# Two heads' 64-column matmuls on the two column halves of the array, and a different order of the down products between two token halves

## The chip, the cores and the metric

The kernel runs on one core of one Trainium2 chip. The metric is the device time of one execution in microseconds (us); lower is better. PE is TensorE (PEld its weight loads), DVE is VectorE, ACT is ScalarE, POOL is GpSimd, SP is SyncE.

## The reference, cut to what matters

One layer of a hybrid decoder for 1024 prompt tokens and 8 decode tokens. After an input projection, half of the channels go through a pooling mixer, the other half through RWKV-7 time mixing, which keeps one 64x64 state S per head (8 heads):

```python
def step(S, inp):
    r_t, w_t, k_t, v_t, aa_t, bb_t = inp
    sa = jnp.einsum('bhvk,bhk->bhv', S, aa_t)
    S = S * w_t[:, :, None, :] + sa[..., None] * bb_t[:, :, None, :] + v_t[..., None] * k_t[:, :, None, :]
    return S, jnp.einsum('bhvk,bhk->bhv', S, r_t)
...
mix = jnp.concatenate([pool_out, rwkv_out], axis=-1).astype(x.dtype) @ w_out
x = x + mix.astype(x.dtype)
h2 = _rmsnorm(x, norm2_g)
x = x + (jnp.square(jax.nn.relu(h2 @ w_up)) @ w_down).astype(x.dtype)
```

A final RMSNorm follows. The widths are 1024 (model) and 4096 (MLP).

## The kernel before

Activations lie transposed, channels on partitions, tokens along the free dimension. There are two stages that matter here.

**The mixer stage** (to about 530 us). The time mixing is done in chunks of 64 tokens. A `Unit` is a pair of heads (`hp`, 0 to 3) and a half of the prompt (512 tokens, 8 chunks), so there are 8 units and 64 chunks. `rkv` and `stage1` prepare a unit, `inverse` inverts its chunks' triangular matrices into `TT`, and `chain` (L578 to L624) walks through its chunks in order, because each chunk needs the state that the chunk before it left in `SV`. In a chunk the two heads of the pair stand in the two halves of the partitions (`R[0]`, `R[1]`). One f32 matmul handles both heads at once: 128 weight columns, 128 moving columns, of which only the two diagonal 64x64 blocks of the result are read. The chain of a chunk is:

1. `pq` (L601) and the first half of `py` (L602) from the state `SV`;
2. ACT copies `pq` to `Q`;
3. `pa` (L605) multiplies `Q` by `TT`;
4. ACT copies the diagonal blocks of `pa` into `SV`, one instruction per head;
5. `pu` (L608) and the second half of `py` (L609);
6. DVE (L617) makes the next chunk's state from `pu`, one instruction per head.

The profile shows every f32 matmul as two passes (x2), each with its own weight load, and every `fp32r` matmul as one. A tuple `128*128` in its rows is the part of the array that an instruction takes (rows*columns). The scheduler mixes other units' matmuls between the chain's: projections (`pj`, fp32r, some 258 columns), `sc` (L431), transposes (`bkt`, L445). The order per engine is fixed when the program is built, and each engine works in that order.

**The MLP stage** (from about 627 us). Half 0 is the first 512 tokens, half 1 the other 520. `up_pair(p)` makes two blocks of the hidden layer with seven products `b0` to `b6` (L1014, 12 matmuls each). Its raw weights `a11`, `a21`, `a22`, `a12` have one buffer each and are loaded by SP (L985); ACT and DVE split them into two fp32r parts (`wh`, `wl`), DVE adds them (L991), adds the products up (L1029), and ACT and DVE write the results `uh`, `ul` (L1025). `down(g, m)` adds one output block of hidden group g (L1080, 12 matmuls `dn` over half 0, 24 over half 1). `downs(G, ...)` is a generator of such blocks; `up_pair` takes one of them after each of its second to fifth product. Groups 0 to 7 belong to half 0, 8 to 15 to half 1. At G == 7, `open_operands(1)` reloads the 14 operand tiles of `up_pair` (520 KB each, queue of POOL) for half 1; a tile is free once half 0's last pair (15) has used it. Group 7's down products need the results of pair 15.

Of the kernel before, what the change touches and what calls it, by code (L numbers as in the profile page):

```python
# [1 line left out]

# [1 line left out]

# [82 lines left out]
def _build(ctx, nc, tc, I, O, dbg):  # L87
# [5 lines left out]
    def act(out, in_, func=AF.Copy, bias=0.0, scale=1.0, **k):  # L93
        A.activation(out, in_, func, bias=bias, scale=scale, **k)  # L94
# [483 lines left out]
    def chain(U):  # L578
        hp = U.hp
        z1 = Zt[U.half][2]  # L580
        for i in range(2):
            nm = f"{hp}_{2 * U.half + i}"
            AR, RB, BKT, SV, TT = U.AR[i], U.RB[i], U.BKT[i], U.SV[i], U.TT
            if i == 0:
                for h in range(2):
                    if U.half == 0:
                        GP.memset(SV[R[h], 0, h, :], 0.0)
                    else:
                        act(SV[R[h], 0, h, :], Sf[hp][R[h], :])
            pyp = ps_y.tile([P, 512], F32, tag="y", name=f"py{nm}")  # L590
            py = pyp.rearrange("p (c h t) -> p c h t", h=2, t=64)
            for c in range(4):
                g = 4 * i + c
                gn = f"{U.nm}_{g}"
                sg = rcp.tile([P, 2, 64], F32, tag="sg", name=f"sg{gn}", bufs=2)
                act(sg, SV[:, c, :, :], scale=U.gam[:, g:g + 1])

                o = 256 * (hp % 2)
                pq, pa = (pcs[:, o + 128 * q:o + 128 * q + 128].rearrange("p (h t) -> p h t", t=64) for q in range(2))
                pu = pq  # L600
                PE.matmul(pq, AR[:, c, 0, :, :], SV[:, c, :, :], start=True, stop=True)  # L601
                PE.matmul(py[:, c, :, :], SV[:, c, :, :], AR[:, c, 1, :, :], start=True, stop=False)  # L602
                Q = rcp.tile([P, 2, 64], F32, tag="Q", name=f"Q{gn}", bufs=2)
                act(Q, pq)
                PE.matmul(pa, TT[:, g, :, :], Q, start=True, stop=True)  # L605
                for h in range(2):
                    act(SV[R[h], c, h, :], pa[R[h], h, :])
                PE.matmul(pu, BKT[:, c, :, :], SV[:, c, :, :], start=True, stop=True)  # L608
                PE.matmul(py[:, c, :, :], SV[:, c, :, :], RB[:, c, :, :], start=False, stop=True)  # L609
                for h in range(2):  # L610
                    if g == 7:
                        dst = Sf[hp][R[h], :]
                    elif c == 3:
                        dst = U.SV[1][R[h], 0, h, :]
                    else:
                        dst = SV[R[h], c + 1, h, :]
                    V.scalar_tensor_tensor(dst, pu[R[h], h, :], U.gam[R[h], g:g + 1], sg[R[h], h, :], ALU.mult, ALU.add)  # L617
            ys = rcp.tile([P, 256], F32, tag="ys", name=f"ys{nm}", bufs=2)
            for h in range(2):
                act(ys[R[h]].rearrange("p (c t) -> p c t", t=64), py[R[h], :, h, :])  # L620
            post(hp, nm, pyp, ys, 256, U.bv[:, 256 * i:256 * i + 256], z1[:, 256 * i:256 * i + 256], ys)
            QM.dma_start(mix_d[4 + hp][U.half][:, 256 * i:256 * i + 256], ys)
        if U.half:
            QM.dma_start(O["wkv_p"][hp], Sf[hp])  # L624
# [484 lines left out]
    for G in range(15):  # L1109
# [6 lines left out]
        if G == 7:  # L1116
            open_operands(1)
            for _ in first:
                pass
        up_pair(2 * G + 2, rest if G == 7 else first)  # L1120
        up_pair(2 * G + 3, () if G == 7 else rest)
        if G == 7:
            for c in (0, 256):
                ss = ps_m.tile([P, 512], F32, tag="m", name=f"ss30{c}")[:, :256]
                acc = tmp(f"acc30{c}", "acc")[:, :256]
# [104 lines left out]
```

## Time and profile before

| what | value |
|---|---|
| time before, median of 3 runs | 1336.7 us (1336.37 to 1336.93) |
| profiled execution, its own time | 1335.81 us |
| its span in the trace | 1334.0 us |
| PE busy | 1267.3 us, 95% |
| DVE busy | 1050.9 us, 79% |
| ACT busy | 822.5 us, 62% |
| mean granted TensorE clock | 0.991 |

A busy share is an average over stages. The matmuls are pipelined: a row's duration runs from its start to its modelled end and overlaps the next one, so the pace of PE is read from the distance between starts, not from durations.

### The profile page before, as it was taken

What the parts mean: (1) busy time and instruction counts of PE and PEld (TensorE: products, weight loads), DVE (VectorE), ACT (ScalarE), POOL (GpSimd) and SP (SyncE); (2) the same over time, 40 slices, a digit from 0 to 9 for tenths busy, and PEclk for the clock granted to TensorE, in tenths of its full rate; (3) what the DMA queues carried; (4) which work ended last, traced back from release to release, by engine and by line L of the source; (5) the groups of instructions that cost most, each with busy time, mean ns of one, the idle gap of its engine ahead of it and who ended that gap; (6) DMA issues with size and microseconds to landing.
All of it is one profiled execution on the core that took longest, in us unless ns stands there. A gap on an engine that the chain in (4) does not pass through costs nothing.

```text
span 1334.0 us, 27179 instructions
## 1 busy us (share of the span) xinstructions
PE 1267.3 (95%) x10230; PEld 1146.4 (86%) x10230; DVE 1050.9 (79%) x2331; ACT 822.5 (62%) x2015; POOL 125.4 (9%) x248
## 2 busy tenths in 40 slices
PE   5999999899999989989999999999899999999996
PEld 5987788798777867789989888998799999999996
DVE  8897687778877756589989997786698787878775
ACT  7668677776777657364757564555465645455552
POOL 4101001210011021110002320001000000000000
PEclk9999999999999989999999999999899999999999
DMA  6323123222222253442335663335634323332321
GB/s 209 102 54 83 43 50 90 95 93 53 66 56 48 63 164 135 142 149 80 119 115 150 181 167 96 113 97 186 217 99 147 103 89 105 94 106 93 104 71 64
DMA packets 119492, 143.19 MB, mean 107 GB/s; under 512 B 55769, under 2 KB 71257, under 8 KB 119353
## 3 DMA queue, kind: packets, MB, share of 16 engines
q1 hardware_dynamic: 97184, 92.22, 23.7%
q0 software_dynamic: 20320, 47.39, 11.4%
q10 hardware_dynamic: 1856, 1.85, 0.4%
q8 instruction: 80, 1.31, 0.4%
q14 instruction: 52, 0.42, 0.1%
HBM read 120.68 MB, written 20.97 MB: 106 GB/s over the span
## 4 chain that ended last, share of the span: by engine, by line
PE 68%; ACT 12%; DVE 11%; DMA 5%; issue 4%; POOL 1%; SPq 0%; DVEq 0%; ACTq 0%; POOLq 0%
PE dn L185 23%; PE b L1014 21%; PE pj L185 8%; PE mx L185 4%; ACT SV L94 2%; DMA a<-in_w_up 2%; PE pcs L608 1%; PE sc L431 1%; ACT wh L94 1%; ACT TT L94 1%; PE pcs L605 1%; DVE tm L525 1%; PE pcs L601 1%; DVE wl L167 1%; PE bkt L445 1%
## 5 line engine op out<-in xcount | busy, mean ns | idle before, releaser
L185 PE MATMUL dn<-uh,wh 128*128 128x260 f32 (+1 forms) x736 | 237.7, 324 | 6.1 <-DVE x L1080 4.3
L185 PE MATMUL dn<-ul,wh 128*128 128x260 f32 (+1 forms) x736 | 237.4, 323 | 1.2 <-DVE ul L1025 1.2
L185 PE MATMUL dn<-uh,wl 128*128 128x260 f32 (+1 forms) x736 | 237.2, 323 | 1.0 <-DVE wl L167 1.0
L94 ACT ACTIVATE wh<-a 128x512 fp32r<-128x512 f32 x192 | 120.8, 629 | 161.3 <-PE dn L185 85.0
L94 ACT ACTIVATE wh<-wr 128x512 fp32r<-128x512 f32 x230 | 142.9, 622 | 98.6 <-PE dn L185 26.0
L185 PE MATMUL pj<-xh,wh 128*128 128x258 f32 (+3 forms) x576 | 172.3, 299 | 13.7 <-ACT wh L94 13.7
L167 DVE TENSOR_TENSOR wl<-wr,wh 128x512 fp32r<-128x512 f32 x230 | 155.7, 681 | 35.4 <-ACT wh L94 27.5
L185 PE MATMUL pj<-xl,wh 128*128 128x258 f32 (+3 forms) x576 | 170.3, 296 | 0.0
L185 PE MATMUL pj<-xh,wl 128*128 128x258 f32 (+3 forms) x576 | 170.0, 295 | 0.1
L185 PEld LDWEIGHTS dn<-uh,wh 128*128 128x128 f32 x736 | 138.9, 189 | 17.3 <-ACT uh L94 3.2
L185 PEld LDWEIGHTS dn<-uh,wl 128*128 128x128 f32 x736 | 138.8, 189 | 12.3 <-DVE wl L167 1.2
L185 PEld LDWEIGHTS dn<-ul,wh 128*128 128x128 f32 x736 | 138.9, 189 | 10.8 <-DVE ul L1025 1.8
L176 DVE TENSOR_TENSOR wl<-a,wh 128x512 fp32r<-128x512 f32 x192 | 131.3, 684 | 6.2 <-ACT wh L94 3.6
L1080 DVE TENSOR_TENSOR x<-dn,x 128x260 f32<-128x260 f32 (+1 forms) x192 | 97.6, 511 | 41.5 <-PE dn L185 39.9
L185 PEld LDWEIGHTS pj<-xh,wh 128*128 128x128 f32 x576 | 109.9, 191 | 17.6 <-ACT wh L94 13.7
L185 PEld LDWEIGHTS pj<-xl,wh 128*128 128x128 f32 x576 | 110.0, 191 | 2.3 <-issue 1.9
L185 PEld LDWEIGHTS pj<-xh,wl 128*128 128x128 f32 x576 | 109.8, 191 | 1.8 <-issue 1.0
L94 ACT ACTIVATE c<-c 128x256 f32<-128x256 f32 (+1 forms) x128 | 53.1, 415 | 45.7 <-DVE c L1029 45.2
L991 DVE TENSOR_TENSOR a<-a,a 128x512 f32<-128x512 f32 x96 | 66.2, 689 | 19.0 <-DMA a<-in_w_up 17.5
L1025 DVE TENSOR_TENSOR ul<-u,uh 128x256 fp32r<-128x256 f32 (+1 forms) x128 | 53.6, 423 | 18.8 <-ACT uh L94 18.4
L185 PE MATMUL mx<-mh,wh 128*128 128x260 f32 (+1 forms) x192 | 64.9, 341 | 3.3 <-ACT mh L94 1.9
L185 PE MATMUL mx<-ml,wh 128*128 128x260 f32 (+1 forms) x192 | 63.6, 332 | 0.9 <-DVE ml L881 0.9
(421 smaller groups left out, 3388.6 us busy)
## 6 DMA issues: line engine op xcount, KB each, us to landing
a<-in_w_up SPq DMA_DIRECT2D x128, 256.0 KB, 2.6
wr<-in_w_down SPq DMA_DIRECT2D x128, 256.0 KB, 2.6
wr<-in_w_in POOLq DMA_DIRECT2D x72, 256.0 KB, 3.1
wr<-in_w_out POOLq DMA_DIRECT2D x26, 256.0 KB, 3.2
xr<-in_xT SPq DMA_DIRECT2D x16, 256.0 KB, 3.6
mr<-mix SPq DMA_DIRECT2D x8, 260.0 KB, 4.3
x<-in_xT SPq DMA_DIRECT2D x4, 520.0 KB, 5.0
blk<-AA SPq DMA_DIRECT2D x16, 128.0 KB, 2.7
```

The lines of the kernel that those rows point to most:

```text
L94: A.activation(out, in_, func, bias=bias, scale=scale, **k)
L167: V.tensor_tensor(l[:, :w], raw[:, :w], f32(h[:, :w]), op=ALU.subtract)
L176: V.tensor_tensor(l, raw, f32(h), op=ALU.subtract)
L185: PE.matmul(ps, lhs, rhs, start=i == 0, stop=i == n - 1)
L431: PE.matmul(psc[:, c, :], BK[:, c, 2 * h:2 * h + 2, :], AR[:, c, :, h, :], start=True, stop=True)
L445: PE.transpose(pt[:, c, :], BK[:, c, 2 * h:2 * h + 2, :].rearrange("p a t -> p (a t)"), ident)
L525: V.tensor_tensor(pr[:, q], l[:, q].unsqueeze(2).to_broadcast([64, m, m, m]), r[:, q].rearrange("p k j -> p j k").unsqueeze(1).to_broadcas ...
L601: PE.matmul(pq, AR[:, c, 0, :, :], SV[:, c, :, :], start=True, stop=True)
L991: V.tensor_tensor(a[out], a[x], a[y], op=op)
L1014: PE.matmul(ps, lhs[:, c], rhs, start=k == i == 0, stop=k == 3 and i == 2)
L1025: V.tensor_tensor(ul, u, f32(uh), op=ALU.subtract)
L1080: V.tensor_tensor(d, ps[:, :n], d, op=ALU.add)
```

## The change

In `chain`, the four matmuls whose result is wanted only on the diagonal are written once per head: the weights are the 64 columns of one head and the result goes to that head's half of the partitions, which is the tile position (0, 0) or (0, 64) of a 128*64 tile. `pa` stays one matmul on the full array with 64 moving columns instead of 128. `Q` and `py` become half as wide, and the output copy `ys` one instruction on 128 partitions instead of two on 64.

In the MLP loop, pair 15 takes only two of group 6's last four down products between its own; the other two follow it. At G == 7 all eight down products of the group come ahead of pair 16, and pairs 16 and 17 run without any. The final norm of half 0 moves from G == 7 to G == 9.

```diff
--- before.py
+++ after.py
@@ -1,4 +1,5 @@
 from contextlib import ExitStack
+from itertools import islice
 
 import numpy as np
 
@@ -588,7 +589,7 @@
                     else:
                         act(SV[R[h], 0, h, :], Sf[hp][R[h], :])
             pyp = ps_y.tile([P, 512], F32, tag="y", name=f"py{nm}")
-            py = pyp.rearrange("p (c h t) -> p c h t", h=2, t=64)
+            py = pyp[:, 0:256].rearrange("p (c t) -> p c t", t=64)
             for c in range(4):
                 g = 4 * i + c
                 gn = f"{U.nm}_{g}"
@@ -596,17 +597,20 @@
                 act(sg, SV[:, c, :, :], scale=U.gam[:, g:g + 1])
 
                 o = 256 * (hp % 2)
-                pq, pa = (pcs[:, o + 128 * q:o + 128 * q + 128].rearrange("p (h t) -> p h t", t=64) for q in range(2))
-                pu = pq
-                PE.matmul(pq, AR[:, c, 0, :, :], SV[:, c, :, :], start=True, stop=True)
-                PE.matmul(py[:, c, :, :], SV[:, c, :, :], AR[:, c, 1, :, :], start=True, stop=False)
-                Q = rcp.tile([P, 2, 64], F32, tag="Q", name=f"Q{gn}", bufs=2)
+                pq, pa, pu = (pcs[:, o + 64 * q:o + 64 * q + 64] for q in range(3))
+                for h in range(2):
+                    PE.matmul(pq[R[h]], AR[:, c, 0, h, :], SV[:, c, h, :], start=True, stop=True)
+                for h in range(2):
+                    PE.matmul(py[R[h], c, :], SV[:, c, h, :], AR[:, c, 1, h, :], start=True, stop=False)
+                Q = rcp.tile([P, 64], F32, tag="Q", name=f"Q{gn}", bufs=2)
                 act(Q, pq)
                 PE.matmul(pa, TT[:, g, :, :], Q, start=True, stop=True)
                 for h in range(2):
-                    act(SV[R[h], c, h, :], pa[R[h], h, :])
-                PE.matmul(pu, BKT[:, c, :, :], SV[:, c, :, :], start=True, stop=True)
-                PE.matmul(py[:, c, :, :], SV[:, c, :, :], RB[:, c, :, :], start=False, stop=True)
+                    act(SV[R[h], c, h, :], pa[R[h]])
+                for h in range(2):
+                    PE.matmul(pu[R[h]], BKT[:, c, h, :], SV[:, c, h, :], start=True, stop=True)
+                for h in range(2):
+                    PE.matmul(py[R[h], c, :], SV[:, c, h, :], RB[:, c, h, :], start=False, stop=True)
                 for h in range(2):
                     if g == 7:
                         dst = Sf[hp][R[h], :]
@@ -614,10 +618,9 @@
                         dst = U.SV[1][R[h], 0, h, :]
                     else:
                         dst = SV[R[h], c + 1, h, :]
-                    V.scalar_tensor_tensor(dst, pu[R[h], h, :], U.gam[R[h], g:g + 1], sg[R[h], h, :], ALU.mult, ALU.add)
+                    V.scalar_tensor_tensor(dst, pu[R[h]], U.gam[R[h], g:g + 1], sg[R[h], h, :], ALU.mult, ALU.add)
             ys = rcp.tile([P, 256], F32, tag="ys", name=f"ys{nm}", bufs=2)
-            for h in range(2):
-                act(ys[R[h]].rearrange("p (c t) -> p c t", t=64), py[R[h], :, h, :])
+            act(ys, pyp[:, 0:256])
             post(hp, nm, pyp, ys, 256, U.bv[:, 256 * i:256 * i + 256], z1[:, 256 * i:256 * i + 256], ys)
             QM.dma_start(mix_d[4 + hp][U.half][:, 256 * i:256 * i + 256], ys)
         if U.half:
@@ -1117,9 +1120,13 @@
             open_operands(1)
             for _ in first:
                 pass
-        up_pair(2 * G + 2, rest if G == 7 else first)
-        up_pair(2 * G + 3, () if G == 7 else rest)
-        if G == 7:
+            for _ in rest:
+                pass
+        up_pair(2 * G + 2, first)
+        up_pair(2 * G + 3, islice(rest, 2) if G == 6 else rest)
+        for _ in rest:
+            pass
+        if G == 9:
             for c in (0, 256):
                 ss = ps_m.tile([P, 512], F32, tag="m", name=f"ss30{c}")[:, :256]
                 acc = tmp(f"acc30{c}", "acc")[:, :256]
```

The built program has 9123 matmuls instead of 8867. In their order PE enters the 128*64 shape 187 times, against 4 times before (the 4 belong to the decode tokens, L705), and leaves it as often.

On PE, a chunk of heads 2 and 3 (unit 1_0, third chunk) before; `sc` is another unit's work:

```order
L431 MATMUL sc2_1_1_1745<-AR1_138,BK_145 128x128
L601 MATMUL pcs_108<-SV1_0_1223,AR2_139 128x128
L602 MATMUL py1_0_1922<-AR2_139,SV1_0_1223 128x128
L431 MATMUL sc2_1_1_1745<-AR1_138,BK_145 128x128
L605 MATMUL pcs_108<-Q1_0_2_1953,TT1_158 128x128
L431 MATMUL sc2_1_1_1745<-AR1_138,BK_145 128x128 x2
L608 MATMUL pcs_108<-SV1_0_1223,BKT1_0_1222 128x128
L609 MATMUL py1_0_1922<-RB2_143,SV1_0_1223 128x128
```

The same chunk in the changed kernel (line numbers are higher by one to three; `pj` and `bkt` are other units' work, `py` with L604 is the first and with L613 the second half of the output):

```order
L604 MATMUL py1_0_1952<-AR2_139,SV1_0_1223 64x64
L446 MATMUL bkt2_1_0_1785<-cst_86,BK_145 128x128 x2
L602 MATMUL pcs_108<-SV1_0_1223,AR2_139 64x64 x2
L604 MATMUL py1_0_1952<-AR2_139,SV1_0_1223 64x64
L186 MATMUL pj15_0_2271<-xh0_171,wl_2268 128x256
...
L446 MATMUL bkt2_1_1_1791<-cst_86,BK_145 128x128
L607 MATMUL pcs_108<-Q1_0_2_1993,TT1_158 128x64
L446 MATMUL bkt2_1_1_1791<-cst_86,BK_145 128x128 x3
L613 MATMUL py1_0_1952<-RB2_143,SV1_0_1223 64x64
L611 MATMUL pcs_108<-SV1_0_1223,BKT1_0_1222 64x64 x2
L613 MATMUL py1_0_1952<-RB2_143,SV1_0_1223 64x64
```

One head's `py` of L604 now stands apart from the group of three behind it, with transposes between, so that the chunk enters the 128*64 shape three times: at the first L604, at L602, and at L613.

On DVE, in pair 15 before (`a..._16` are raw weights of pair 16, `x10<-dn6_5` adds a down product of group 6):

```order
L176 TENSOR_TENSOR wl_11984<-a22_15_11786,wh_11983 128x512
L1080 TENSOR_TENSOR x10_6510<-dn6_5_0_11883,x10_6510 128x512
L176 TENSOR_TENSOR wl_12008<-a12_15_11788,wh_12007 128x512
L991 TENSOR_TENSOR a21_16_12144<-a21_16_12144,a22_16_12146 128x512
L1029 TENSOR_TENSOR u3_15_11914<-u2_15_11875,b3_15_11897 128x256
L167 TENSOR_TENSOR wl_12061<-wr_12058,wh_12060 128x512
L1080 TENSOR_TENSOR x10_6510<-dn6_6_0_11922,x10_6510 128x512
L167 TENSOR_TENSOR wl_12081<-wr_12078,wh_12080 128x512
L1029 TENSOR_TENSOR u4_15_11953<-u2_15_11875,b4_15_11936 128x256
```

The same place in the changed kernel:

```order
L177 TENSOR_TENSOR wl_12184<-a22_15_12026,wh_12183 128x512
L994 TENSOR_TENSOR as3_16_12494<-a11_16_12462,a21_16_12464 128x512
L1083 TENSOR_TENSOR x10_6750<-dn6_4_0_12084,x10_6750 128x512
L177 TENSOR_TENSOR wl_12208<-a12_15_12028,wh_12207 128x512
L1032 TENSOR_TENSOR u2_15_12115<-p1_15_12047,b2_15_12098 128x256
L994 TENSOR_TENSOR a21_16_12464<-a21_16_12464,a22_16_12466 128x512
L168 TENSOR_TENSOR wl_12233<-wr_12230,wh_12232 128x512
L1083 TENSOR_TENSOR x10_6750<-dn6_5_0_12123,x10_6750 128x512
L168 TENSOR_TENSOR wl_12253<-wr_12250,wh_12252 128x512
L1032 TENSOR_TENSOR u3_15_12154<-u2_15_12115,b3_15_12137 128x256
```

The addition that needs `a22_16` still stands among pair 15's additions, between `u2` and `u3`. The split of `a22_15`, whose end frees the buffer for `a22_16`, has moved ahead of `as3_16`, the addition that needs `a21_16` (before it stood behind it), and four rows lie between it and the addition of `a22_16` instead of two.

On DVE, the end of pair 15 before (`x10<-dn7_0` is the first use of group 7's first down product):

```order
L1025 TENSOR_TENSOR ul31_11781<-u10_15_12001,uh31_11780 128x256
L1029 TENSOR_TENSOR c12_15_12023<-u4_15_11953,b6_15_12006 128x256
L176 TENSOR_TENSOR wl_12171<-a12_16_12148,wh_12170 128x512
L991 TENSOR_TENSOR a12_16_12148<-a12_16_12148,a11_16_12142 128x512
L1025 TENSOR_TENSOR ul30_11779<-u01_15_12025,uh30_11778 128x256
L1080 TENSOR_TENSOR x10_6510<-dn7_0_0_12064,x10_6510 128x512
```

And in the changed kernel:

```order
L1032 TENSOR_TENSOR c12_15_12223<-u4_15_12173,b6_15_12206 128x256
L168 TENSOR_TENSOR wl_12361<-wr_12358,wh_12360 128x512
L1083 TENSOR_TENSOR x10_6750<-dn6_6_0_12236,x10_6750 128x512
L168 TENSOR_TENSOR wl_12381<-wr_12378,wh_12380 128x512
L1028 TENSOR_TENSOR ul30_12019<-u00_15_12073,uh30_12018 128x256
L1028 TENSOR_TENSOR ul30_12019<-u01_15_12225,uh30_12018 128x256
L1028 TENSOR_TENSOR ul31_12021<-u11_15_12177,uh31_12020 128x256
L1028 TENSOR_TENSOR ul31_12021<-u10_15_12201,uh31_12020 128x256
L1083 TENSOR_TENSOR x10_6750<-dn6_7_0_12256,x10_6750 128x512
L168 TENSOR_TENSOR wl_12401<-wr_12398,wh_12400 128x512
L1083 TENSOR_TENSOR x10_6750<-dn7_0_0_12304,x10_6750 128x512
```

Two down products of group 6 and the splits of further down weights now lie between the last sum `c12` of pair 15 and group 7's first down product; two additions for pair 16 no longer do.

## Rows read from the trace of the kernel before

**Rows 1.** the first line of the page: the profiled execution's span.

```profile
span 1334.0 us, 27179 instructions
```

**Rows 2.** busy time by stage; (x) counts instructions; last columns clock, DMA share, GB/s.

```profile
66.00:530.00 464.00, 436.75 (x4281) 370.00 (x4280) 350.28 (x858) 334.77 (x957) 57.17 (x116) 0.99 0.29 78
...
640.00:940.00 300.00, 298.41 (x1864) 267.09 (x1864) 247.66 (x496) 175.74 (x385) 35.25 (x67) 1.00 0.47 141
...
1030.00:1300.00 270.00, 269.99 (x2252) 269.74 (x2251) 212.15 (x428) 147.45 (x305) 0.00 (x0) 1.00 0.31 96
```

**Rows 3.** timeline of PE over one chunk: start us, duration us, instruction, xcount.

```profile
151.32 0.43 PE L601 MATMUL pcs<-SV,AR 128*128 128x128 f32 x2
...
151.81 0.39 PE L431 MATMUL sc<-AR,BK 128*128 128x128 f32 x2
152.13 0.49 PE L605 MATMUL pcs<-Q,TT 128*128 128x128 f32 x2
152.46 0.61 PE L431 MATMUL sc<-AR,BK 128*128 128x128 f32 x4
153.16 0.49 PE L608 MATMUL pcs<-SV,BKT 128*128 128x128 f32 x2
153.48 0.39 PE L609 MATMUL py<-RB,SV 128*128 128x128 f32 x2
...
153.95 0.60 PE L445 MATMUL bkt<-cst,BK 128*128 128x128 f32 x4
...
154.51 0.39 PE L601 MATMUL pcs<-SV,AR 128*128 128x128 f32 x2
```

**Rows 4.** instructions on tile pcs on ACT: duration ns min/median/max.

```profile
L94 ACT ACTIVATE SV<-pcs x128: 197/219/222, 106.7 to 519.7; 64x64 f32<-64x64 f32 x128
...
L94 ACT ACTIVATE Q<-pcs x64: 254/278/287, 68.0 to 518.4; 128x128 f32<-128x128 f32 x64
```

**Rows 5.** timeline of PE around 16 matmul passes that use 64 columns.

```profile
533.65 0.39 PE L185 MATMUL mx<-mh,wh 128*128 128x512 f32 x1
533.88 0.40 PE L185 MATMUL mx<-ml,wh 128*128 128x512 f32 x1
534.20 1.09 PE L705 MATMUL dpa<-r,dS 128*64 128x2 f32 x16
535.23 0.50 PE L185 MATMUL mx<-mh,wl 128*128 128x512 f32 x1
535.56 0.40 PE L185 MATMUL mx<-mh,wh 128*128 128x512 f32 x1
```

**Rows 6.** timeline of weight loads: those of the same 16 passes.

```profile
534.20 1.01 PEld L705 LDWEIGHTS dpa<-r,dS 128*64 128x64 f32 x16 [0.36 <-ACT dX L94]
```

**Rows 7.** timeline of weight loads: 32 passes that alternate between two 32x32 tiles.

```profile
102.00 0.58 PEld L565 LDWEIGHTS pi<-XB,AA 32*32 32x32 f32 x32 [0.86 <-DVE XB L560]
```

**Rows 8.** instructions on tile ys: the two copies of a segment's output.

```profile
L94 ACT ACTIVATE ys<-py x32: 364/379/381, 119.0 to 521.2; 64x256 f32<-64x256 f32 x32
```

**Rows 9.** timeline of PE before group 7's down products; [idle before <-releaser].

```profile
941.78 0.47 PE L185 MATMUL dn<-uh,wh 128*128 128x512 f32 x1 [0.67 <-DVE x L1080]
...
945.45 0.48 PE L185 MATMUL dn<-uh,wh 128*128 128x512 f32 x1 [2.04 <-DVE x L1080]
...
949.76 1.22 PE L185 MATMUL dn<-uh,wh 128*128 128x512 f32 x2 [1.78 <-ACT uh L94]
...
953.06 0.39 PE L185 MATMUL dn<-uh,wl 128*128 128x512 f32 x1
```

**Rows 10.** timeline of DVE ahead of that: its two longest pauses.

```profile
931.55 0.69 DVE L991 TENSOR_TENSOR as<-a,a 128x512 f32<-128x512 f32 x1 [4.57 <-issue]
...
939.41 0.69 DVE L991 TENSOR_TENSOR a<-a,a 128x512 f32<-128x512 f32 x1 [5.03 <-DMA a<-in_w_up]
```

**Rows 11.** busy time by stretch around that place.

```profile
920.00:950.00 30.00, 25.51 (x146) 21.56 (x145) 17.50 (x34) 13.68 (x29) 7.42 (x14) 0.93 1.01 336
...
960.00:990.00 30.00, 30.00 (x207) 27.89 (x206) 25.47 (x50) 19.13 (x41) 0.00 (x0) 1.00 0.27 84
```

## The prediction, on record before the changed kernel ran

> **What bounds the kernel now.** The profiled execution took 1335.8 us by its own time, 0.9 us under the median of the runs; its span is 1334.0 us [rows 1]. I read first where PE, the engine with the highest busy share, is really paced by its own work, and for that the busy time by stage [rows 2]. From 1030 to 1300 us PE is busy for all of 270 us with 2252 passes, 0.12 us each: nothing there can be gained by moving other engines' work. The same holds almost wholly from 640 to 940. In the mixer stage, 66 to 530 us, PE's row says 437 of 464 us busy, but matmul durations overlap, and this share hides lost time. So I went to the timeline of one chunk of the chain [rows 3] and counted starts. A pass of 128 f32 columns paces at (0.61 - 0.39)/2 = 0.11 us (rows with x4 and x2). The chunk lasts from one L601 to the next, 3.19 us. Against that pace PE loses 0.05 us between L601 and the `sc` passes behind L602 (0.49 for four passes), 0.10 ahead of L605 (0.32 for two), 0.11 in L605, 0.26 ahead of L608 (0.70 for four) and 0.10 in L608: 0.62 us. These are waits of the chain, for `Q`, for the copies into `SV` and for weight loads that cannot run ahead of an operand that isn't there. Over 64 chunks that is some 40 us. The third place is the gap ahead of group 7's down products [rows 9].
>
> **The change, part 1: the chain.** Four terms.
>
> *Matmul time.* Now ten passes a chunk, 10 x 0.11 = 1.10 us. After: 16 passes of 64 columns and two of `pa`, which load 128 weight columns each as before and keep 0.11. The trace has 64-column passes: 16 of them have their weight loads within 1.01 us [rows 6], so some 0.06 us each, all on the same half of the columns. If the halves run in line, a chunk has 16 x 0.06 + 0.22 = 1.18 us, 5 us more over 64 chunks. If every pass overlaps with one of the other half, 0.48 + 0.22 = 0.70, 26 us less. Tiles do overlap where they differ in rows and in columns: 32 loads of 32 columns that alternate between two such tiles take 0.58 us [rows 7], 0.018 each, where half of 0.06 would be 0.03. Halves of the columns with the same rows are not in the trace. The order rows show how much can overlap: of eight matmuls a chunk only the two of L602 stand directly side by side for both heads; one L604 stands alone, and L613, L611, L611, L613 come as head 0, 0, 1, 1, so that only their middle can overlap. That is about 0.18 us less than in line, 1.00 us, or 6 us less than now. I take this, -6, and keep -26 and +5 as ends.
>
> *Changes of shape.* PE enters the `128*64` shape 183 times more, and leaves it as often. Around the 64-column passes that exist [rows 5] the pace of the matmuls ahead is 0.23 us; the first pass starts 0.32 us behind the last of them, 0.09 late. Behind the last pass the next matmul starts some 0.08 us late (16 x 0.06 from 534.20 is 535.16, it starts at 535.23) and the one behind it after 0.33 instead of 0.23, 0.10 late. A round trip costs 0.27 us: nothing of the next shape, not even its weights, seems to start until the passes of the old one are through. 183 x 0.27 = +49 us.
> The Trainium skill (TensorEngine Tiling (Array Packing), Key Properties) says that a change of tiling mode drains TensorE, while a change of tile within a mode does not; the trace agrees as far as it goes, with 0.27 us. It states no price, and it speaks against an order that enters the mode three times a chunk.
>
> *Waits that this replaces.* The 0.62 us a chunk was waiting for the chain. The steps get shorter: `Q` copies 64 columns instead of 128, which by the `SV` copy of that width is 0.22 instead of 0.28 us [rows 4]; a 64-column result is complete some 0.05 us sooner, four times a chunk; and the first L613 and L611 need only head 0's copy, 0.22 us ahead of head 1's. That is 0.4 us or more, and the changes of shape themselves fill the rest: 183/64 of them are 0.77 us a chunk, in the places where PE waited. I count 39 of the 40 us as gone; if half of the waits stay, it is 20. So the change trades waits for drains, one for one. On ACT and DVE no instruction gets something new to wait for.
>
> *The output copy.* Two copies of 0.38 us a segment [rows 8] become one of about the same length, ahead of a matmul that PE runs into directly: 16 x 0.38 = 6 us at most; other work covers part of it, and I take -3.
>
> Sum of part 1: -6 + 49 - 39 - 3 = +1 us.
>
> **Part 2: the gap.** Before group 7's down products PE stood idle for 0.67 + 2.04 + 1.78 us, and then ran at the lower of its two clock levels (1.2 instead of 2.4 GHz; the mean granted clock of 920 to 950 us is 0.93 [rows 11]): from 945.45 to 953.06 us 14 passes start, which at 0.23 need 3.2 us; without the 1.78 of idle they took 5.8 [rows 9]. Together 4.5 + 2.6 = 7.1 us. The cause stands on DVE: it waited 4.57 and 5.03 us at the two additions for pair 16 [rows 10], whose weights came late while the operand reload filled the DMA engines (share 1.01, 336 GB/s [rows 11]); pair 15's additions are queued behind them. After, two down products, 24 passes of 0.23 = 5.6 us, lie behind pair 15's last product, and DVE splits `a22_15`, which frees the buffer for the late load, ahead of the first of those additions. In line, 5.6 us of cover and a load asked for earlier by more than the 4.57 us of that first pause are more than the 4.5 us of idle time. The clock then has no reason to fall. I take -7. If DVE is held up as long as before and the drain comes anyway, it is 0. The weights of pair 17 are asked for behind ten down weights on SP, but PE has 22 us of down products there, and DVE kept up with pair 17 alone before: PE without a gap from 960 to 990, DVE 25.5 of 30 us busy [rows 11]. The final norm of half 0 is the same work two groups later; I cost it at nothing, and 2 us either way if it meets PE differently.
>
> **Sum.** 1335.8 + 1 - 7 = 1329.8 us for the profiled execution, 1330.7 beside the median; I say 1330.
>
> **The rivals.**
> - *All halves overlap.* Then matmul time is -26 instead of -6: 1310 us. For it: the two 32-column tiles [rows 7]. Against it: the order, with heads 0, 0, 1, 1. Chance 0.15.
> - *Halves in line.* Matmul time +5 instead of -6: 1341 us. For it: passes of one half pace at 0.06, and two halves would need both weights and moving columns from the same rows at once, which no row shows. Chance 0.13. The Trainium skill (TensorE: Matmul & The Clock Gate, Part 3, The mechanism) says that weight loads overlap matmuls in flight only where the row groups differ, which would be this case; no row here shows column halves.
> - *Drains on top of the waits: slower.* A drain ahead of the chain's own matmul delays the chain, so the next wait comes later instead of vanishing. If half of the 40 us stays, the time is 1350 us. It decides from a price of 0.31 us a round trip with all waits gone (6 us over 183), or from 6 us of waits that stay. For it: three entries a chunk where one would do. Chance 0.17.
> - *The gap stays*, because DVE is held by the same two additions: part 2 is 0, 1337 us, the change would not do what its order says. Chance 0.07.
> - The forecast, 1330, within 1322 to 1338: chance 0.48.
>
> **How the numbers follow.** 0.2% is 2.7 us, about what a measurement of this kernel can tell. Faster (under 1334): 0.40 of the forecast's 0.48 and all of the first rival, 0.55. Same: 0.05 of the forecast, the gap's 0.07 and 0.03 of the halves in line, 0.15. Slower: the rest of these two, 0.13, and the drains, 0.17, together 0.30. The range reaches to the overlap's 1310 and to the drains' 1350, 1311 to 1349, and leaves the outer halves of both out.
>
> **What would show it.** In the trace after: the pace of the two L602 passes by head (0.06 in line, 0.03 overlapped); the gap between the last `pj` ahead of L604 and L604, and between L613 and the `pj` behind it (0.09 and 0.18 over pace); waits at L607 and L611 near nothing; the mixer stage's end near 530 us; no idle PE and full clock between pair 15 and pair 16; DVE's two pauses short. Wrong it is if the stage ends 10 us or more to either side, which would mean that drains are dearer or are hidden, or that halves overlap in another way than the order lets me think.

## The result, and the profile after

| | before | after |
|---|---|---|
| median of 4 runs | 1336.8 us (1336.4 to 1337.4) | 1345.1 us (1343.5 to 1347.3) |
| ratio | | 1.0063, 95% interval 1.0045 to 1.0080 |
| profiled execution, span | 1335.8, 1334.0 us | 1343.9, 1342.1 us |

The change made the kernel 0.6% slower, 8.4 us by the ratio. The forecast was 1330.

Where the time went is read from the start of the MLP stage. First the up projection's first and last product in the changed kernel, then in the kernel before (instructions of one line: duration in ns, first and last start in us):

```profile
L1017 PE MATMUL b<-x11h,wh x128: 279/281/472, 624.2 to 1285.3; 128*128 128x256 f32 x64, 128*128 128x260 f32 x64
```

```profile
L1014 PE MATMUL b<-x11h,wh x128: 278/281/473, 615.2 to 1277.3; 128*128 128x256 f32 x64, 128*128 128x260 f32 x64
```

All that comes ahead of the MLP got 9.0 us longer, and from the first to the last product the kernel is 1.0 us shorter (661.1 for 662.1). By these two executions part 1 lost the time, and part 2 hardly gained any.

The chain in the changed kernel, timeline of PE as in [rows 3]. From here on q is the product `pq` (now L602), y the first half of `py` (L604), a `pa` (L607), u `pu` (L611) and Y the second half of `py` (L613):

```profile
153.34 0.43 PE L607 MATMUL pcs<-Q,TT 128*128 128x64 f32 x2
153.61 0.66 PE L432 MATMUL sc<-AR,BK 128*128 128x128 f32 x4
154.31 0.34 PE L611 MATMUL pcs<-SV,BKT 128*64 128x64 f32 x4
154.48 0.29 PE L613 MATMUL py<-RB,SV 128*64 128x64 f32 x4
...
155.38 0.38 PE L446 MATMUL bkt<-cst,BK 128*128 128x128 f32 x2
155.69 0.33 PE L604 MATMUL py<-AR,SV 128*64 128x64 f32 x2
155.95 0.44 PE L446 MATMUL bkt<-cst,BK 128*128 128x128 f32 x2
156.32 0.34 PE L602 MATMUL pcs<-SV,AR 128*64 128x64 f32 x4
156.49 0.28 PE L604 MATMUL py<-AR,SV 128*64 128x64 f32 x2
156.70 0.39 PE L186 MATMUL pj<-xh,wl 128*128 128x256 f32 x1
...
157.39 0.33 PE L607 MATMUL pcs<-Q,TT 128*128 128x64 f32 x2
157.56 0.50 PE L446 MATMUL bkt<-cst,BK 128*128 128x128 f32 x3
```

Two things are to be seen. The four passes of both heads (L602, 0.34 us) take hardly longer than two passes of one head (L604, 0.33 us), and the two heads' passes start 0.007 us apart: the halves of the columns run at the same time. And head 0's y goes out by itself at 155.69, 0.6 us ahead of q, between two pieces of other work: that is one entry into the half shape more. In PE's order the two heads' y stand apart in 55 of the 64 chunks and the two heads' Y in 45; the chain enters the half shape 183 times.

The copies, as [rows 4] and [rows 8], came out as counted on: `Q` 223 ns instead of 278, one `ys` copy of 384 ns for two of 379.

```profile
L95 ACT ACTIVATE Q<-pcs x64: 196/223/225, 68.5 to 538.2; 128x64 f32<-128x64 f32 x64
```

```profile
L95 ACT ACTIVATE ys<-py x16: 383/384/388, 120.3 to 540.6; 128x256 f32<-128x256 f32 x16
```

The gap, as [rows 9 to 11]: PE, then DVE, then busy time by stretch (PE, PEld, DVE, ACT, POOL, clock, DMA share, GB/s).

```profile
954.60 0.77 PE L186 MATMUL dn<-uh,wh 128*128 128x512 f32 x1 [3.48 <-DVE x L1083]
955.16 0.63 PE L186 MATMUL dn<-ul,wh 128*128 128x512 f32 x1
...
959.86 0.53 PE L186 MATMUL dn<-uh,wh 128*128 128x512 f32 x1
960.22 0.39 PE L186 MATMUL dn<-ul,wh 128*128 128x512 f32 x1
```

```profile
940.03 0.69 DVE L994 TENSOR_TENSOR as<-a,a 128x512 f32<-128x512 f32 x1 [5.87 <-DMA a<-in_w_up]
...
951.18 0.69 DVE L168 TENSOR_TENSOR wl<-wr,wh 128x512 fp32r<-128x512 f32 x1 [3.83 <-ACT wh L95]
```

```profile
920.00:950.00 30.00, 30.00 (x190) 27.02 (x190) 19.03 (x37) 13.34 (x27) 7.40 (x14) 1.00 0.71 238
930.00:960.00 30.00, 26.52 (x146) 22.90 (x145) 16.22 (x32) 13.70 (x30) 7.40 (x14) 0.89 1.01 351
...
1030.00:1300.00 270.00, 267.86 (x2225) 266.91 (x2224) 216.99 (x445) 146.07 (x306) 0.00 (x0) 1.00 0.32 102
```

The two downs run where PE stood in the kernel before, but PE stops 3.48 us a little later, the clock falls again (passes 0.43 us apart from 955.16 on, 0.23 at the end), and DVE still pauses 5.87 us for up weights and 3.83 us for down weights. The stretch from 1030 us on, without a gap in [rows 2], now lacks 2.1 us: there the final norm stands.

### The profile page after: what moved, and what is told of

It reads as the page before. It is cut to its first block, busy times and chain, and to the rows that moved or that the text cites. A ratio compares the mean times of both kernels' runs of the same rounds, so it can differ in the third digit from the quotient of the medians.

```text
span 1342.1 us, 28241 instructions
## 1 busy us (share of the span) xinstructions
PE 1284.4 (96%) x10742; PEld 1145.7 (85%) x10742; DVE 1048.9 (78%) x2331; ACT 811.8 (60%) x1999; POOL 125.0 (9%) x248
## 3 DMA queue, kind: packets, MB, share of 16 engines
q0 software_dynamic: 20320, 47.39, 11.1%
## 4 chain that ended last, share of the span: by engine, by line
PE 75%; DVE 9%; ACT 7%; DMA 5%; issue 2%; POOL 1%; SPq 0%; DVEq 0%; ACTq 0%; POOLq 0%
PE dn L186 23%; PE b L1017 19%; PE pj L186 15%; PE mx L186 4%; PE sc L432 2%; PE py L604 1%; DMA a<-in_w_up 1%; PE py L613 1%; PE pcs L602 1%; PE bkt L446 1%; ACT TT L95 1%; PE pcs L611 1%; ACT wh L95 1%; DVE x L1089 1%; DMA mr<-mix 1%
## 5 line engine op out<-in xcount | busy, mean ns | idle before, releaser
L186 PE MATMUL pj<-xh,wl 128*128 128x258 f32 (+3 forms) x576 | 173.1, 301 | 0.1
L186 PEld LDWEIGHTS dn<-ul,wh 128*128 128x128 f32 x736 | 139.1, 189 | 10.7 <-DVE ul L1028 1.6
L1083 DVE TENSOR_TENSOR x<-dn,x 128x260 f32<-128x260 f32 (+1 forms) x192 | 98.2, 513 | 43.3 <-PE dn L186 41.9
```

The lines of the kernel that those rows point to most:

```text
L186: PE.matmul(ps, lhs, rhs, start=i == 0, stop=i == n - 1)
L1083: V.tensor_tensor(d, ps[:, :n], d, op=ALU.add)
```

## The experiments

**Theories.** A: the chain loses by its entries into the half shape. B: the loss is in part 2. C: the chain's own round trip (from the state through the products and copies to the next state) sets the pace, whatever the entries. D: it is a wait for the pool's weights that the new order brings. For the price of an entry: it replaces a wait (the step on record), or comes on top. For part 2, E: the reload's load on the DMA engines keeps the gap; G: DVE's own order does. Each result is given as ratio to the kernel before with its 95% interval; a difference in us is that ratio's, or of two medians of one set of runs where it says so.

**The parts by themselves.** Part 1 alone is the chain of the diff, part 2 alone the rest of it.

> Part 1 alone: the halves in the chain, the order of the down products as before. If the loss sits in the chain (theory A: the trace of the changed kernel has the first product of the up projection 9.0 us later than before, and takes that to be the chain's own loss), about 1346 us, +9 over the kernel before. By the sum on record (+1 for part 1) about 1338. If the loss were in the other part (theory B), 1337 or less.

Measured: 1350.4 us, 1.0086 (1.0070 to 1.0102), +11.5 us.

> Part 2 alone: the chain as before, the eight down products by themselves and two kept for the gap. By the sum on record -7, about 1330 us. By what the trace of the changed kernel shows after its first up product (706.1 us to the end against 707.1), about -1, 1336. If part 2 is what loses (theory B), 1345.

Measured: 1336.2 us, 0.9974 (0.9962 to 0.9987), -3.5 us. The two add up to +8.0, the whole change measured +8.4. Part 1 is the loss, B falls, and part 2 gains half of its 7 us.

**Fewer entries.** y queued behind q, Y behind u:

```diff
                 for h in range(2):
-                    PE.matmul(pq[R[h]], AR[:, c, 0, h, :], SV[:, c, h, :], start=True, stop=True)
-                for h in range(2):
-                    PE.matmul(py[R[h], c, :], SV[:, c, h, :], AR[:, c, 1, h, :], start=True, stop=False)
+                    mq = PE.matmul(pq[R[h]], AR[:, c, 0, h, :], SV[:, c, h, :], start=True, stop=True)
+                with tc.issue_after(mq.ins):
+                    for h in range(2):
+                        PE.matmul(py[R[h], c, :], SV[:, c, h, :], AR[:, c, 1, h, :], start=True, stop=False)
...
-                    PE.matmul(pu[R[h]], BKT[:, c, h, :], SV[:, c, h, :], start=True, stop=True)
-                for h in range(2):
-                    PE.matmul(py[R[h], c, :], SV[:, c, h, :], RB[:, c, h, :], start=False, stop=True)
+                    mu = PE.matmul(pu[R[h]], BKT[:, c, h, :], SV[:, c, h, :], start=True, stop=True)
+                with tc.issue_after(mu.ins):
+                    for h in range(2):
+                        PE.matmul(py[R[h], c, :], SV[:, c, h, :], RB[:, c, h, :], start=False, stop=True)
```

> Part 1 alone, with y queued behind q and Y behind u on TensorE, so that no half of y or Y goes out by itself: the chain enters the other shape 127 times in place of 181. Theory A (each entry and return costs TensorE some 0.27 us plus the pass beside it, and the 54 lone entries are what turned a gain into a loss): some 27 us less than part 1 alone if nothing takes their place, 1319 us; 1330 if half of it comes back as waits. Rival C (the chain's own round trip of products and copies sets the pace, and TensorE's entries lie in its waits): no less than part 1 alone, 1344 to 1348, since queueing y behind q can only hold it up.

Measured: 1331.0 us, 0.9939 (0.9920 to 0.9958), -8.2 us, and 19.4 us less than part 1 alone by the medians. In PE's order in the built programs the half shape is entered 131 times more than in the kernel before, and 183 times more in part 1 alone (the expectation has 127 and 181). Its timeline shows the pairs together, L602 being L601 here:

```profile
154.26 0.34 PE L601 MATMUL pcs<-SV,AR 128*64 128x64 f32 x4
154.42 0.29 PE L604 MATMUL py<-AR,SV 128*64 128x64 f32 x4
154.64 0.38 PE L185 MATMUL pj<-xh,wh 128*128 128x256 f32 x1
```

> Part 1 alone, but y and Y stay whole passes of 128 columns on the full array, as before; only q and u go in halves. 128 entries into the other shape, 64 times 2 passes of 128 columns more than in the changed chain (0.055 us each, +7 us). Theory A: 1326 us (-27 +7 beside part 1 alone), up to 1335 if half comes back as waits. Rival C: 1344 to 1348.

Against part 1 alone the edit is this one; `py` and the two copies of `ys` stay as in the kernel before:

```diff
-                for h in range(2):
-                    PE.matmul(py[R[h], c, :], SV[:, c, h, :], AR[:, c, 1, h, :], start=True, stop=False)
+                PE.matmul(py[:, c, :, :], SV[:, c, :, :], AR[:, c, 1, :, :], start=True, stop=False)
...
-                for h in range(2):
-                    PE.matmul(py[R[h], c, :], SV[:, c, h, :], RB[:, c, h, :], start=False, stop=True)
+                PE.matmul(py[:, c, :, :], SV[:, c, :, :], RB[:, c, :, :], start=False, stop=True)
```

Measured: 1340.3 us, 1.0009 (0.9994 to 1.0023), +1.2 us. It has 133 entries more than the kernel before. C falls: with the same steps and 52 or 50 entries fewer than part 1 alone the kernel is 19 and 10 us faster.

> The kernel before, whole passes, with y queued behind q and Y behind u; no halves. If the ordered chain's gain over part 1 alone is the entries that it saves (theory A): nothing to save here, ratio 1.000 within 0.002. If the order by itself shortens the chain: down to 0.994.

Measured: 1338.1 us, 0.9994 (0.9983 to 1.0005). The order alone gives nothing, so the ordered chain's gain is that of halves without lone entries (groups of one head's passes alone).

**The pool's weights.** The traces show a stop that the kernel before hasn't got there; PE in the changed kernel:

```profile
221.82 1.02 PE L786 MATMUL po<-d,pw 128*128 128x256 f32 x4
226.84 2.05 PE L786 MATMUL po<-d,pw 128*128 128x256 f32 x4 [3.99 <-DMA pw<-in_pool_w]
```

A second buffer takes that wait away:

```diff
-        pw_sb = pp.tile([P, P], F32, tag="pw", name=f"pw{g}_{half}")
+        pw_sb = pp.tile([P, P], F32, tag="pw", name=f"pw{g}_{half}", bufs=2)
```

> The kernel before with one thing else: two buffers in place of one for the pool's 64 KB weights `pw`, the control of the next run. In the kernel before PE waits once for such a load, 4.4 us, near 477 us, and runs some 5 us slower behind it at a granted clock below 1. Theory D (such a wait costs its length and the low clock behind it): 4 to 9 us less than before, ratio 0.993 to 0.997. Theory A (only the chain's entries matter): no change in this kernel, ratio 1.000.

Measured: 1337.7 us, 0.9994 (0.9982 to 1.0005).

> The changed kernel with two buffers for `pw`. Its trace has what the kernel before has not: at 222.8 us PE stands for 4.0 us between two `po` products that have come to stand side by side, since the second one's weights go into the one buffer that the first reads, and the granted clock is 0.89, 0.95 and 0.93 in the three stretches of 15 us from 225 on (3.5 us of lost time). Theory D (this wait is most of the 8.2 us that were lost): the kernel comes down by more than the control does, 8 to 12 us, to a ratio of about 0.998 to 1.000, at most 4 us above the control. Theory A (the loss is the chain's entries alone): still 8 us above the control, wherever that is.

Measured: 1355.0 us, 1.0114 (1.0094 to 1.0135). PE no longer waits for `pw`, and the time is not shorter but 7 us longer than the changed kernel's by the two ratios. The clock stands beside this: the mean granted clock of the six runs is 0.972 to 0.987. But the run at 0.987, the clock of the changed kernel's profiled run, took 1347.5 us, 8.3 above its kernel before, so at that clock too the missing wait gives nothing. D falls as the explanation. Its busy time by stretch has the clock at the lower of its two levels for 30 us, where the chain runs with little beside it:

```profile
240.00:270.00 30.00, 28.44 (x166) 21.26 (x164) 15.97 (x40) 17.41 (x50) 6.42 (x13) 0.50 0.24 80
```

In the changed kernel the stretch behind that place had 0.92 in the mean, in the kernel before it 1.00; first the row of after, then that of before:

```profile
225.00:270.00 45.00, 41.48 (x472) 31.94 (x472) 31.30 (x78) 32.21 (x96) 10.20 (x20) 0.92 0.41 125
```

```profile
225.00:270.00 45.00, 40.48 (x423) 33.16 (x421) 32.00 (x79) 37.51 (x113) 10.61 (x21) 1.00 0.37 118
```

This is no accident of one execution: in this stretch all eleven profiles of kernels with the whole chain show 1.00, and all nine with halves in the chain less: 0.85 in part 1 alone, 0.81 in the ordered chain, 0.89 with y and Y whole, 0.61 here, 0.85 to 0.97 in the others. The changed chain lowers the clock there. With two buffers the clock fell even though PE no longer waited for `pw`; what lowers it was not found.

> The changed kernel, both parts, with y queued behind q and Y behind u. From part 1 so ordered (ratio 0.994) and part 2 alone (0.997), if they add: 0.991, 1325 to 1328 us where before takes 1337 to 1339.

Measured: 1331.2 us, 0.9944 (0.9931 to 0.9957). It beats both kernels, but part 2 gives the ordered chain nothing beyond its -8.2: the two do not add, and why is not shown.

> The same with two buffers for `pw`. In the ordered chain PE waits for `pw` 3.0 and 1.4 us, and the granted clock from 210 to 255 us is 0.90, 0.76 and 0.70 (9.6 us of lost time). Theory D: 8 to 14 us less than without the second buffer, ratio 0.981 to 0.985. Theory A: no more than the control gains.

Measured: 1332.6 us, 0.9960 (0.9947 to 0.9973): no gain by the second buffer here either.

**The price of an entry.** A product that nobody reads, behind each up product, in the half shape or in the full one (`pf` is the up product's own result tile, in columns that it leaves free):

```diff
+            PE.matmul(pf[0:64, 320:384], h[:, 0:64], X[x][0][:, 0, 0:64], start=True, stop=True)
```

```diff
+            PE.matmul(pf[:, 320:384], h[:, 0:128], X[x][0][:, 0, 0:64], start=True, stop=True)
```

> The kernel before with one pass of 64 columns in the half shape (128x64) behind each of the 224 up products, where PE has work without a wait; the passes' results are not used. This is the price of a change of shape by itself: by the sum on record 0.27 us a round trip, 60 us over 224 above the control. By the lone blocks of the changed kernel's chain (0.35 us in the median, 0.12 of it two passes) 0.24, 54 us. If a change of shape costs nothing where no wait lies beside it: the same time as the control.

> The control: the same 224 passes with 128 columns of weights, in the shape of the passes around them. 224 passes of 64 columns, by the 64-column passes of the chain 0.06 us each: 13 us over the kernel before, 15 at most.

Measured: 1362.2 us, 1.0168 (1.0144 to 1.0191), and the control 1361.5 us, 1.0169 (1.0147 to 1.0191). The change of shape costs nothing here. PE and its weight loads (PEld) in the half run:

```profile
1099.99 0.28 PE L1015 MATMUL b<-x11h,wl 128*128 128x260 f32 x1
1100.12 0.19 PE L1016 MATMUL b<-x11h,wh 128*64 128x64 f32 x1
1100.14 0.36 PE L1015 MATMUL b<-x21h,wh 128*128 128x260 f32 x1
1100.34 0.28 PE L1015 MATMUL b<-x21l,wh 128*128 128x260 f32 x1
```

```profile
1099.99 0.14 PEld L1016 LDWEIGHTS b<-x11h,wh 128*64 128x64 f32 x1
1100.12 0.19 PEld L1015 LDWEIGHTS b<-x21h,wh 128*128 128x128 f32 x1
```

The half pass's weights are loaded beside the pass ahead of it, 0.13 us early.

> The ordered chain with a product of two passes in the half shape put directly ahead of each of the 64 `a` products, waiting for the same `Q` and with a result that is not used: 59 more entries, each at a matmul that waits. If changes of shape take the place of the waits, as the sum on record has it, no more than 5 us over the control. If they come on top of the waits: 59 times 0.24 to 0.27, 14 to 16 us over the control.

> The control of the run before: the same 64 products with 128 columns of weights, so without a further change of shape. Two passes of 64 columns each, 0.12 us, 7 us over the ordered chain if they come on top of the waits too: 1338 us, ratio 0.999.

Here `ident` and `Q` are the operands, both f32, and `a` is queued behind the product. Measured: 1352.5 us, 1.0102 (1.0084 to 1.0120), and the control 1341.4 us, 1.0027 (1.0010 to 1.0044): 11.1 us between the medians over 61 entries (196 for 135 in PE's order; the expectation has 59), 0.18 us each, though PE waits at that place. The mean granted clock of the runs is 0.983 and in the control 0.986; by the slope of 1 us for 0.001 (below, an estimate) some 2.6 us of the 11.1 are the clock's, and 0.14 us each is left. The control stands 11.8 us above the ordered chain by the ratios, where 7 was expected. What sets this apart from the up products is the type, so they were run with f32 products (`ident` on both sides):

> As the run with 224 lone passes of the half shape behind the up products, but the added product is f32 (two passes of 64 columns, constants on both sides) as in the chain. If the price of a change of shape belongs to f32 passes: 0.19 to 0.27 us each over the control, 43 to 60 us. If it belongs to the chain's waits and not to the type: the control's time.

> The control: the same 224 f32 products in the shape around them. Two passes of 0.06 us and a next pass held up by its weight load as in the f32r control (0.10 us each in all there): 0.16 to 0.25 us each, 36 to 56 us over the kernel before.

Measured: 1425.8 us, 1.0655 (1.0631 to 1.0678), and the control 1382.6 us, 1.0332 (1.0309 to 1.0355): 43.2 us over 224, 0.19 us each. And on the operands of the f32r runs, read as f32:

> The 224 lone products of the half shape once more, on the up product's own operands as in the f32r run, but read as f32, two passes each. If it is the type that has a change of shape cost 0.19 us: 43 us over its control, about 1426 us. If it was the constant operand: the control's time within 5 us.

> The control, with 128 columns of weights in the shape around it: as the f32 control with constants, about 1383 us.

Measured: 1425.5 us, 1.0652 (1.0627 to 1.0677), and 1380.4 us, 1.0326 (1.0307 to 1.0345): 45.0 us, 0.20 each. It is the type, with the two passes that f32 takes here for one of f32r. PE and then PEld with f32 constants in the half shape, and below them both views of the control:

```profile
1102.27 0.28 PE L1015 MATMUL b<-xt3h,wl 128*128 128x260 f32 x1
1102.48 0.33 PE L1016 MATMUL b<-cst 128*64 128x64 f32 x2
1102.73 0.39 PE L185 MATMUL dn<-uh,wh 128*128 128x260 f32 x1
1102.96 0.28 PE L185 MATMUL dn<-ul,wh 128*128 128x260 f32 x1
```

```profile
1102.47 0.19 PEld L1016 LDWEIGHTS b<-cst 128*64 128x64 f32 x2
1102.73 0.19 PEld L185 LDWEIGHTS dn<-uh,wh 128*128 128x128 f32 x1
```

```profile
1101.78 0.28 PE L1015 MATMUL b<-xt2h,wl 128*128 128x260 f32 x1
1101.90 0.33 PE L1016 MATMUL b<-cst 128*128 128x64 f32 x2
1102.04 0.37 PE L185 MATMUL dn<-uh,wh 128*128 128x260 f32 x1
1102.24 0.28 PE L185 MATMUL dn<-ul,wh 128*128 128x260 f32 x1
```

```profile
1101.78 0.31 PEld L1016 LDWEIGHTS b<-cst 128*128 128x128 f32 x2
1102.01 0.19 PEld L185 LDWEIGHTS dn<-uh,wh 128*128 128x128 f32 x1
```

In the control the product's first weight load stands 0.12 us ahead of its first pass, and the pass comes on pace. In the half shape it stands beside the pass, the pass comes 0.09 us late, and the full shape behind it waits for its weights in the same way: from the last f32r pass to the second one behind, 0.69 us for 0.46.

**The gap.** Part 2 alone, with half of the reload:

```diff
-                for t, d in zip(XO[half][i], XD[i]):
-                    GP.dma_start(t, d)
+                GP.dma_start(XO[half][i][0], XD[i][0])
+                XO[half][i] *= 2
```

> Part 2 alone with half of the reload: of each operand of half 1 only the high part is brought back, and the products read it in place of the low part, which is left out. If it is the reload's load on the DMA engines that makes the weights late and keeps the gap (theory E): DVE's pauses of 3.9 and 4.1 us at 929 and 942 us go, PE does not stop between 930 and 960 and the clock stays up there: 4 to 6 us less than part 2 alone, ratio 0.993 to 0.995. If the gap comes from DVE's own order of work (theory G): the time of part 2 alone, 0.997.

Measured: 1331.7 us, 0.9947 (0.9929 to 0.9964), 3.6 us better than part 2 alone by the ratios, of which the intervals leave little sure. Its busy time by stretch, DVE's longest pause and PE's only stop there, and below them stretch and stop of part 2 alone:

```profile
930.00:960.00 30.00, 28.34 (x145) 23.25 (x144) 21.21 (x40) 13.09 (x27) 2.12 (x4) 1.00 0.60 191
```

```profile
930.89 0.69 DVE L992 TENSOR_TENSOR as<-a,a 128x512 f32<-128x512 f32 x1 [5.03 <-DMA a<-in_w_up]
```

```profile
944.17 0.47 PE L186 MATMUL dn<-uh,wh 128*128 128x512 f32 x1 [1.58 <-DVE x L1081]
```

```profile
930.00:960.00 30.00, 27.41 (x130) 22.80 (x130) 18.05 (x35) 11.72 (x24) 4.23 (x8) 0.89 0.85 299
```

```profile
945.22 0.77 PE L186 MATMUL dn<-uh,wh 128*128 128x512 f32 x1 [2.59 <-DVE x L1081]
```

PE's stop falls from 2.59 to 1.58 us, and 1.58 is less than in any of the five profiles with this order of the downs and the whole reload (2.59 to 4.57 us). DVE's pause for the up weights is no shorter (5.03 us, 3.88 in part 2 alone), so half of the reload does not bring those weights sooner. E is shown in part at most. In this profile the clock stays up (1.00 for 0.89), but the length of the stop does not settle that. The ordered chain with both parts has the same order of the downs and stops for longer than part 2 alone, at a full clock:

```profile
930.00:960.00 30.00, 27.06 (x121) 21.32 (x120) 18.64 (x36) 12.80 (x27) 2.12 (x4) 1.00 0.67 236
```

```profile
939.54 0.47 PE L186 MATMUL dn<-uh,wh 128*128 128x512 f32 x1 [2.87 <-DVE x L1085]
```

The kernel before with ordered y and Y, which has the old order of the downs, stops for 2.04 and 2.69 us and has 1.00 in this stretch too, where the kernel before has 0.89. So the clock's part in the gap differs between profiles of the same order of the downs, and how much of the 3.6 us is the reload's is open.

## Why the prediction was wrong

**The step that failed is "waits that this replaces", -39 of 40 us, and in it the sentence that the changes of shape themselves fill the rest.** An entry added at a matmul that waits anyway costs 0.18 us more than its control (0.14 without the clock's part), not much less than the 0.19 to 0.20 where nothing waits; inside the wait it would have cost nothing. The rival "drains on top of the waits" named this. Some of the waits did go: counted from starts at full clock as in [rows 3], PE loses 0.14 us in the mean ahead of a in the kernel before and 0.06 in part 1 alone.

**A second thing was put at nothing: the clock.** The changed chain lowers it between 225 and 270 us. The prediction has no term for it. What it costs is an estimate from runs of one kernel: with y and Y whole, three runs at 0.986 to 0.987 have spans of 1334 to 1335 us, four at 0.982 1338 to 1340, so 1 us for 0.001 (a line through all twelve runs has the same slope, the runs of the ordered chain 0.9, of the kernel before 0.7). The mean granted clock over the runs is 0.986 for part 1 alone, 0.984 for the ordered chain and for y and Y whole, and 0.989 for the kernel before beside them.

The table adds up what the runs price and shows what they leave for the waits. Matmul time is an estimate from the distances between starts: before, ten passes of 0.11, 70 us over 64 chunks; after, four pairs of heads at 0.123 and a at 0.11, 39 us; and a pair whose heads stand apart is counted with 0.11 more, 55 y and 45 Y in part 1 alone.

| kernel | matmul time | entries x 0.193 | sum | measured | of it the clock | left for the waits |
|---|---|---|---|---|---|---|
| part 1 alone | -32 + 100 x 0.11 = -21 | 183: +35 | +14 | +11.5 (9.4 to 13.7) | +3 | -6 |
| ordered chain | -32 | 131: +25 | -7 | -8.2 (-10.7 to -5.6) | +5 | -6 |
| y and Y whole | -20 | 133: +26 | +6 | +1.2 (-0.8 to +3.1) | +5 | -10 |

With the prediction's own price of 0.27 for an entry the last column is -20, -16 and -20. Either way about half of the -39 or less.

- *Matmul time, -6 with ends -26 and +5*: -21. The mechanism that was given to a rival, "all halves overlap", holds: four passes in the time of two. I had let only the order L613, L611, L611, L613 speak, which overlaps in its middle; q and u go out as pairs in 62 and 64 of the 64 chunks. And a's two passes on 64 moving columns start 0.055 us apart where nothing holds them up; the prediction let them keep 0.11.
- *Changes of shape, 183 x 0.27 = +49*: the count held, and so did the price as it was meant, over the pace of the passes: 86.5 us over 224 lone f32 products is 0.39 each, and less two passes of 0.06 that is 0.27. But a product in the full shape pays some 0.08 of it in the same place (43.3 us over 224 is 0.19, less the same passes), so the shape itself adds 0.19, +35. The 40 us of waits were counted over the pace too and so hold such costs of the kernel before.
- *The output copy, -3*: no run has it by itself. The kernel with y and Y whole keeps the two copies and leaves -10 in the table, the two with one copy -6, so nothing speaks for a gain.
- *The gap, -7*: -3.5. PE's idle time shrank, but a new stop of 3.48 us (2.59 in part 2 alone) came behind the two downs and in both profiles the clock fell as before. That "a load asked for earlier by more than the 4.57 us of that first pause" would do is the sentence that failed: the pause for pair 16's weights stayed (5.87 us, 3.88 in part 2 alone). And the 2.6 us for the clock are no firm part of the gap, since in either order of the downs some profile has it at 1.00 there (2.04 and 2.69 us of stops in the old order, 2.87 in the new). The final norm at no cost held: PE lacks 2.8 us around it before (990 to 1030 us, 37.25 of 40 busy) and 2.2 after (1080 to 1130 us, 47.85 of 50).

So part 1 went from +1 to +12, in the prediction's own terms, by -15 for the passes, +19 for the waits, +3 for the copy and +3 for the clock, with the rest in the rounding. Two rivals came true at once, and it is luck that the one hid a good part of the other: without the overlap the loss would have been larger. The sign was decided by the term for which no row showed an entry beside a wait.

The Trainium skill (TensorEngine Tiling (Array Packing), Key Properties) says that a change of tiling mode drains TensorE. For f32 the runs agree, with 0.19 to 0.20 us a round trip over the same product in the full shape; for f32r they show no cost. The Trainium skill (TensorE: Matmul & The Clock Gate, Part 3, The mechanism) has weight loads overlap matmuls in flight only where row groups differ. Here halves with the same rows and other columns ran four passes in 0.34 us for two in 0.33, and in the ordered chain head 1's weights load at 154.261, beside head 0's pass from 154.256 on, so the measurement goes against it.

**What stays open.** The table's last column is what the other columns leave, so each of their errors is in it: the cost of the clock is a slope, and the 0.11 for heads that stand apart is an estimate. Why the clock falls with the changed chain, why it stayed down for 30 us in the run with two `pw` buffers, why the two parts do not add, and what makes the up weights late with half of the reload, was not found.

## What to carry to other kernels

Splitting a small f32 product over halves of the columns pays only if the halves go out as pairs and the shape is entered seldom: count the entries in the order on the engine, at about 0.2 us each here, against some 0.1 us for each pass that is saved. A stall that one sees beside a new cost is not a credit against it until a run has shown the one inside the other. A clock that falls in one profile is no property of the kernel until several profiles show it: here it was one between 225 and 270 us and none at the gap. And where a queue frees work head by head, the scheduler sends out the half that is ready first; keeping it behind its partner was worth 19 us.

## What the runs showed of the hardware

- Passes of 64 columns on the two halves of the columns, with the same rows, overlap almost wholly (0.34 us for four passes, 0.33 for two).
- A change between the full and the half shape and back costs, over the same product in the full shape, 0.19 to 0.20 us in f32 and nothing measurable in f32r (1362.2 for 1361.5 us over 224). At a matmul that waits anyway it costs 0.18 us (0.14 without the clock's part, an estimate). With f32r the weights of the other shape are loaded 0.13 us ahead of the pass, with f32 they are not.
- One short f32r pass of 64 columns costs 0.10 us (22.6 us over 224) although the next pass starts 0.02 to 0.03 us behind it: the pass after that comes only 0.20 us later, for a pace of 0.12.
- With halves in the chain the granted clock between 225 and 270 us is 0.61 to 0.97 in all nine profiles, with the whole chain 1.00 in all eleven.
